# First sums staged in block tiles, and a weight add moved from VectorE to an accumulating DMA, in a Strassen-type feed-forward layer

## Chip, cores and metric

One core of a Trainium2 chip. The metric is the device time of one execution in microseconds; the time before is the median of 3 runs.

## What is computed (the reference, shortened)

One decoder layer on x of 512 tokens by 2048 features, in float32: a token mixer (gated linear attention beside differential attention), then a gated feed-forward with a causal convolution of width 3. The change touches only the feed-forward, and of it the passage from the up to the down projection and the down projection itself:

```python
def conv_ffn(h, w_ffn_in, conv_w, conv_b, w_ffn_out):    # h: (1, 512, 2048)
    up = h @ w_ffn_in                                    # 2048 x 11264
    a, b = up[..., :5632], up[..., 5632:]
    a = causal_conv3(a, conv_w) + conv_b
    return (gelu(a) * b) @ w_ffn_out                     # 5632 x 2048
x = x + rmsnorm(conv_ffn(rmsnorm(x, g2), ...), g3)
```

## The kernel before

**Products in two halves.** Every float32 operand is split in two: ScalarE copies it into a float32r tile (the high half, `whi`), VectorE subtracts that from the operand (the low half, `wlo`). A product is three matmuls: high by high, high by low, low by high. Weights are loaded, split and used in granules of 128 x 1024 words (512 KB); `granule` (line 116) does the split, on lines 125 and 126. The split tiles are a ring of six, three granules.

**Seven products for eight.** Both projections are cut into units that use a Strassen-type scheme: a unit has seven products instead of eight, named x0, z0, y0, z1, x1, y1, y2, each of two granules. Its weights are sums of blocks of the weight matrix, its other operands sums of blocks of activations. `class Unit` (line 209) runs them. `self.t` (two tiles tagged `rt`, a ring of four) holds block (0,0) for x0; then `more` (line 226) adds block (0,1) with an accumulating DMA from POOL, for z0; then VectorE adds block (1,1), which lies in `self.b22`, on line 267, for y0; then VectorE adds block (1,0), which lies in `self.b21`, on line 291, for y2. `self.b22` (two tiles tagged `raw`, also a ring of four) is read by z1, gets block (0,1) by another pair of accumulating DMAs, and is then `self.e`, for y1. `self.b21` is read by x1 and by the add on line 291.

**Units.** The up projection has 20 Strassen units (line 1376), the down projection 10 (`down_unit`, line 1356; two halves of the columns for each of five pairs of groups). The order of TensorE's work interleaves neighbours: y0, z1, x1, y1 of a unit, x0 of the next, y2 of the unit, z0 of the next. An up granule is 24 matmuls of 256 columns, a down granule 12 of 512 columns.

**Activation sums.** The down units read sums of activation blocks (a11, s5, s2, s3, a12, s7, a22), which the up stage has written to DRAM. `stage` (line 1331) loads one of them into a tile `st` of the pool `ff`; `prepare` (line 1335) splits it into a place in `ah` and `al` (lines 138 and 139), where the up stage's activations lay. For the first pair of groups this happens in the last up unit (lines 1384 to 1411). The pool `ff` takes the space of `sums`, whose last reader is z1 of that unit, so a tile `st` is free only then.

**Outputs.** A unit's product lies in PSUM banks; `into` (line 1350) takes it into the accumulators: ScalarE copies on line 1352 for the first pair of groups, VectorE adds on line 1354 for the others. x0's product is collected apart, in `accp`, and added to three quarters of the accumulators at the start of `last_group` (lines 1482 to 1487), twelve adds of 128 x 512. After it come the last group's plain products (lines 1470 to 1472), the norm and the output.

**Order.** Outside the stretches under `manual_schedule`, a list scheduler orders each engine's instructions when the kernel is built: it takes what is ready by its own estimate of time, the earlier line of the program first. Adds and loads can therefore run well ahead of the place in which they are written. All plain loads are issued on SP's queue, accumulating DMAs on POOL's; both queues are in order. `step` (line 95) takes work from the list `fill` after a granule, at a rate that `pace` sets.

Of the kernel before, what the change touches and what calls it, by code (L numbers as in the profile page):

```python
# [9 lines left out]
F32 = mybir.dt.float32  # L10
# [3 lines left out]
ALU = mybir.AluOpType  # L14
# [3 lines left out]
P = 128  # L18
# [12 lines left out]
GR = 1024  # L31
# [6 lines left out]
def hybrid_layer(ctx: ExitStack, tc: tile.TileContext, x, attn_pre_norm, w_in, w_alpha_up, b_alpha,  # L38
# [52 lines left out]
    fill = []  # L91
# [14 lines left out]
    def drain():  # L106
        while fill:
            for _ in fill.pop(0):
                pass
# [99 lines left out]
    class Unit:  # L209
        def __init__(self, a, block, prods, chain, out, narrow=True):  # L210
            self.narrow = narrow
            self.a, self.block, self.prods, self.chain, self.out = a, block, prods, chain, out
            self.banks, self.b22, self.b21, self.t, self.x_done = {}, None, None, None, False

# [8 lines left out]
                self.prods(self.banks[c], op, g, hl, seg[1] == "0")  # L223
                step()

        def more(self, raws, j):
            for g in range(2):
                nc.gpsimd.dma_start(out=raws[g].rearrange("p (a b) -> p a b", a=self.a),  # L228
                                    in_=self.block(0, j, g), accum_op=ALU.add)

        def ahead(self):
            self.e = [room["rt"].tile([P, GR], F32, name="rt", tag="rt", bufs=4) for _ in range(2)]
# [30 lines left out]
        def y0(self):  # L263
            if self.b22 is None:
                self.fetch()
            for g in range(2):
                tt(self.t[g], self.t[g], self.b22[g], ALU.add)
            self.run("y0", "s2", self.t)
            self.out("y0", self.banks["y"])

        def z1(self):
# [15 lines left out]
        def y1(self):  # L287
            self.run("y1", "s7", self.e)
            self.out("y1", self.banks["y"])
            for g in range(2):  # L290
                tt(self.t[g], self.t[g], self.b21[g], ALU.add)

        def y2(self):
# [1034 lines left out]

    staged = {}

    def stage(c, n):
        raw = staged[c, n] = ff.tile([P, GR], F32, name="st", tag="st", bufs=4)
        dma(raw, sd[c][n].rearrange("p g x -> p (g x)"))

    def prepare(c, n):
        if (c, n) not in staged:
            stage(c, n)
        split(piece(ah, *place[n]), piece(al, *place[n]), staged.pop((c, n)))
# [11 lines left out]
    def into(dst, b, sign, first):  # L1350
        if first:
            act(dst, b, AF.Copy, scale=float(sign))
        else:
            tt(dst, dst, b, ALU.add if sign > 0 else ALU.subtract)

    def down_unit(c, cb):
        def block(i, j, g):
            gi = 2 * c + 1 + g
            col = 1024 * cb + 512 * j
            return w_y3[:, 4 * gi + 2 * i:4 * gi + 2 * i + 2, col:col + 512]  # L1360

        def chain(ch):
            return [bank(psm if ch == "x" else psa) for _ in range(2)]

        def out(seg, b):
            for j in range(2):
                if seg == "x0":
                    into(accp[j][:, 512 * cb:512 * (cb + 1)], b[j], 1, c == 0)
                    continue
                half, col, sign = {"z0": (1, 1, 1), "y0": (0, 1, -1), "z1": (0, 1, 1), "x1": (0, 0, 1),  # L1370
                                   "y1": (1, 1, -1), "y2": (1, 0, 1)}[seg]
                into(quarter(acc[2 * half + j], 2 * cb + col), b[j], sign, c == 0 and seg in ("z0", "y0", "x1", "y2"))

        return Unit(2, block, down_prods, chain, out, narrow=False)

    ups = [up_unit(gi, br) for gi in range(1, NG) for br in range(2)]
    for i, u in enumerate(ups):
        nxt = ups[i + 1] if i + 1 < len(ups) else None
        if i == 0:
            u.x0()  # L1380
            u.z0()
        u.y0()
        u.z1()
        if nxt is None:
            sums.close()
            ff = ctx.enter_context(tc.tile_pool(name="ff", bufs=2, reuse_waits="tile"))
            for n in ("a11", "s5", "s2", "s3"):
                stage(0, n)
        if i == 0:
            for h, r in enumerate(s7raw):  # L1390
                split(up["s7"][0][:, h], up["s7"][1][:, h], r)
        if nxt is None:
            prepare(0, "a11")
            stage(0, "a12")
        u.x1()
        if nxt is None:
            prepare(0, "s5")
            stage(0, "s7")
        u.y1()
        if nxt is not None:  # L1400
            nxt.x0()
            u.y2()
            nxt.z0()
        else:
            downs = [down_unit(c, cb) for c in range(NG // 2) for cb in range(2)]
            prepare(0, "s2")
            stage(0, "a22")
            downs[0].x0()
            prepare(0, "s3")
            downs[0].fetch()  # L1410
            u.y2()
    accp = [ff.tile([P, D // 2], F32, name=f"accp{j}", bufs=1) for j in range(2)]
# [7 lines left out]
    def quarter(v, c):  # L1420
        return v[c // 2][:, 512 * (c % 2):512 * (c % 2 + 1)]
# [58 lines left out]
        eng.tensor_tensor(a, a, quarter(g3, c), ALU.mult)  # L1480

    def last_group(gi, us):
        for j in range(2):
            for half, c, op in ((1, 0, ALU.add), (1, 1, ALU.subtract), (0, 1, ALU.subtract)):
                for b in range(2):
                    dst = quarter(acc[2 * half + j], 2 * b + c)
                    tt(dst, dst, accp[j][:, 512 * b:512 * (b + 1)], op)
        for c in range(2):
            gr = ffn_out_weights(gi, c)
            for t in range(NT):  # L1490
                ffn_out_part(us, gr, t, c)
                gain(t, c, nc.vector)

        rs = {}
        x1 = {t: v[:, h].rearrange("p k c -> p (k c)").bitcast(F32)
              for t, (v, h) in enumerate(((ah, 1), (al, 1), (ah, 2), (al, 2)))}
        for t in range(NT):
            dma(x1[t], x1d[t])

        def finish(t, *ps):  # L1500
            for i in ps:
                sl = slice(512 * i, 512 * (i + 1))
                a = quarter(acc[t], i)
                stt(a, a, rs[t], x1[t][:, sl], ALU.mult, ALU.add)
                if t == 3:
                    dma(out2[t * P:(t + 1) * P, sl], a)
                elif i % 2:
                    sl = slice(512 * i - 512, 512 * (i + 1))
                    dma(out2[t * P:(t + 1) * P, sl], acc[t][i // 2])

        with tc.manual_schedule(engines=IN_ORDER):
            gr = [ffn_out_weights(gi, c) for c in (2, 3)]
            for t in range(NT):
                ffn_out_part(us, gr[0], t, 2)
                gain(t, 2, nc.gpsimd if t < 3 else nc.vector)
                if t:
                    finish(t - 1, 0, 1, 2)
                ffn_out_part(us, gr[1], t, 3)
                if t:
                    finish(t - 1, 3)  # L1520
                gain(t, 3, nc.vector)
                ss = small.tile([P, 1], F32, name="ss", tag="ss")
                nc.vector.reduce_sum(ss, ssf[t], axis=AX.X)
                rs[t] = rsqrt_mean(ss, D)
            finish(3, 0, 1, 2, 3)
# [40 lines left out]
```

## Time and profile before

| | |
|---|---|
| median of 3 runs | 2111.48 us (2108.53 to 2116.08) |
| the profiled execution | 2112.14 us, its span 2110.4 us |
| TensorE matmul busy | 2069.4 us (98%) |
| TensorE weight loads busy | 1892.6 us (90%) |
| VectorE busy | 1555.2 us (74%) |
| ScalarE busy | 967.9 us (46%) |
| DMA moved | 353.31 MB, mean 167 GB/s |

The last up unit's y2 and the first down unit's x0 lie at 1652 to 1665 us; the down units end near 2056, the output at 2110. In the rows below PE is TensorE, DVE VectorE, ACT ScalarE, POOL GpSimd and SP SyncE; a q behind an engine's name is its queue of DMA issues. L126 is line 126.

### The profile page before, as it was taken

The page shows a single profiled execution, that of the slowest core. Times are in us where ns is not written, and L with a number is a line of the kernel's source. Part 1 is how long each engine was busy: PE and PEld are TensorE (multiplying, and loading weights), DVE is VectorE, ACT ScalarE, POOL GpSimd, SP SyncE. Part 2 cuts the span into 40 slices and gives each one's busy share as a digit, 9 for nine tenths or more (in the row PEclk, how much of TensorE's full clock was granted, in tenths as well). Part 3 has the DMA queues.
Part 4 walks back from the last instruction along what each step waited for, and adds up shares of the span by engine and source line. Part 5 has one row for each costly group of instructions (what it writes and reads, how often), then busy time and mean ns, then how long its engine had stood idle before and what let it go on. Part 6 is the DMA issues. An engine that isn't in the chain of part 4 may idle for free.

```text
span 2110.4 us, 34792 instructions
## 1 busy us (share of the span) xinstructions
PE 2069.4 (98%) x14161; PEld 1892.6 (90%) x14161; DVE 1555.2 (74%) x1873; ACT 967.9 (46%) x1247; POOL 248.1 (12%) x281
## 2 busy tenths in 40 slices
PE   7999999999999999999999999999999999999997
PEld 5899999888888889899999999999999788887886
DVE  7957667577873255887787877878778777988887
ACT  4445444444553234454544444454455564444433
POOL 2010111111110000011111011111111110111101
PEclk9999999999999999999999999999999999999999
DMA  9376675844455245447667677577675876775753
GB/s 309 104 172 165 159 170 137 274 126 144 148 160 202 95 150 170 116 114 185 161 140 189 147 170 185 128 172 171 151 175 145 261 209 173 193 195 151 190 151 138
DMA packets 255269, 353.31 MB, mean 167 GB/s; under 512 B 14128, under 2 KB 185572, under 8 KB 253316
## 3 DMA queue, kind: packets, MB, share of 16 engines
q1 hardware_dynamic: 184260, 268.24, 37.4%
q0 software_dynamic: 70848, 82.85, 25.0%
q8 instruction: 111, 1.82, 0.3%
q14 instruction: 50, 0.41, 0.1%
HBM read 303.33 MB, written 47.71 MB: 166 GB/s over the span
## 4 chain that ended last, share of the span: by engine, by line
PE 32%; issue 22%; DVE 3%; DMA 2%; POOL 2%; ACT 0%; POOLq 0%; DVEq 0%; SPq 0%; ACTq 0%
PE bank L320 6%; PE bank L319 6%; PE bank L318 6%; PE bank L1346 3%; PE bank L1347 3%; PE bank L1348 3%; PE bank L164 1%; PE bank L163 1%; PE bank L162 1%; DMA rt<-in_w_ffn_out_dram 1%; DVE wlo L126 1%; POOL rt L228 1%; POOL raw L228 1%; PE bank L1471 0%; PE bank L1472 0%
## 5 line engine op out<-in xcount | busy, mean ns | idle before, releaser
L125 ACT ACTIVATE whi<-raw 128x1024 fp32r<-128x1024 f32 x283 | 298.9, 1061 | 494.6 <-PE bank L319 164.8
L126 DVE TENSOR_TENSOR wlo<-raw,whi 128x1024 fp32r<-128x1024 f32 x283 | 343.6, 1220 | 231.5 <-ACT whi L125 228.1
L125 ACT ACTIVATE whi<-rt 128x1024 fp32r<-128x1024 f32 x306 | 322.8, 1060 | 357.9 <-PE bank L319 198.6
L126 DVE TENSOR_TENSOR wlo<-rt,whi 128x1024 fp32r<-128x1024 f32 x306 | 373.1, 1221 | 141.9 <-ACT whi L125 132.8
L318 PE MATMUL bank<-ah,whi 128*128 128x256 f32 x1600 | 442.0, 276 | 0.9 <-DVE u L352 0.9
L320 PE MATMUL bank<-ah,wlo 128*128 128x256 f32 x1600 | 442.1, 276 | 0.3 <-DVE wlo L126 0.3
L319 PE MATMUL bank<-al,whi 128*128 128x256 f32 x1600 | 441.9, 276 | 0.0
L318 PEld LDWEIGHTS bank<-ah,whi 128*128 128x128 f32 x1600 | 300.4, 188 | 1.4 <-issue 1.0
L320 PEld LDWEIGHTS bank<-ah,wlo 128*128 128x128 f32 x1600 | 300.3, 188 | 0.8 <-DVE wlo L126 0.8
L319 PEld LDWEIGHTS bank<-al,whi 128*128 128x128 f32 x1600 | 300.3, 188 | 0.1
L1347 PE MATMUL bank<-wlo,ah 128*128 128x512 f32 x560 | 219.2, 391 | 1.4 <-DVE wlo L126 1.4
L1346 PE MATMUL bank<-whi,ah 128*128 128x512 f32 x560 | 213.7, 392 | 6.2 <-ACT whi L125 3.0
L1348 PE MATMUL bank<-whi,al 128*128 128x512 f32 x560 | 218.2, 390 | 0.0
L181 PE MATMUL bank<-whi,ah 128*128 128x512 f32 x448 | 184.5, 414 | 0.0
L182 PE MATMUL bank<-wlo,ah 128*128 128x512 f32 x448 | 175.2, 391 | 1.0 <-DVE wlo L126 0.8
L183 PE MATMUL bank<-whi,al 128*128 128x512 f32 x448 | 175.1, 392 | 0.0
L1346 PEld LDWEIGHTS bank<-whi,ah 128*128 128x128 f32 x560 | 105.2, 188 | 30.4 <-ACT whi L125 6.1
L1347 PEld LDWEIGHTS bank<-wlo,ah 128*128 128x128 f32 x560 | 105.5, 188 | 25.7 <-DVE wlo L126 4.0
L1348 PEld LDWEIGHTS bank<-whi,al 128*128 128x128 f32 x560 | 105.4, 188 | 21.7
L318 PE MATMUL bank<-s5h,whi 128*128 128x256 f32 x400 | 110.7, 277 | 1.1 <-ACT whi L125 1.0
L320 PE MATMUL bank<-s5h,wlo 128*128 128x256 f32 x400 | 110.6, 277 | 0.8 <-DVE wlo L126 0.8
L320 PE MATMUL bank<-s2h,wlo 128*128 128x256 f32 x400 | 110.8, 277 | 0.0
(283 smaller groups left out, 4406.9 us busy)
## 6 DMA issues: line engine op xcount, KB each, us to landing
raw<-in_w_ffn_in_dram SPq DMA_DIRECT2D x96, 512.0 KB, 5.2
raw<-in_w_in_dram SPq DMA_DIRECT2D x64, 512.0 KB, 4.6
raw<-in_w_ffn_out_dram SPq DMA_DIRECT2D x48, 512.0 KB, 5.6
rt<-in_w_ffn_in_dram SPq DMA_DIRECT2D x40, 512.0 KB, 5.8
rt<-in_w_ffn_in_dram POOLq DMA_DIRECT2D x40, 512.0 KB, 5.9
raw<-in_w_ffn_in_dram POOLq DMA_DIRECT2D x40, 512.0 KB, 7.0
raw<-in_w_o_dram SPq DMA_DIRECT2D x32, 512.0 KB, 3.8
rt<-in_w_ffn_out_dram SPq DMA_DIRECT2D x20, 512.0 KB, 8.3
```

What stands on the lines that cost most here:

```text
L125: act(hi, raw, AF.Copy)
L126: tt(lo, raw, hi.bitcast(F32), ALU.subtract)
L181: mm(banks[t], ah[:, t, s, :], w[0][:, k, :], start=st, stop=False)
L182: mm(banks[t], ah[:, t, s, :], w[1][:, k, :], start=False, stop=False)
L183: mm(banks[t], al[:, t, s, :], w[0][:, k, :], start=False, stop=sp)
L228: nc.gpsimd.dma_start(out=raws[g].rearrange("p (a b) -> p a b", a=self.a), in_=self.block(0, j, g), accum_op=ALU.add)
L318: mm(o, wh, sh[:, :, kk, :], start=start and kk == 0 and n == 0, stop=False, **NOW)
L319: mm(o, wh, sl[:, :, kk, :], start=False, stop=False, **NOW)
L320: mm(o, wl, sh[:, :, kk, :], start=False, stop=kk == HK - 1, **NOW)
L1346: mm(b[j], sh[:, o:o + P], w[0][:, q, :], start=start and st == 0, stop=False, **NOW)
L1347: mm(b[j], sh[:, o:o + P], w[1][:, q, :], start=False, stop=False, **NOW)
L1348: mm(b[j], sl[:, o:o + P], w[0][:, q, :], start=False, stop=st == 3, **NOW)
```

## The change

Three things. (1) In the last up unit, a11 and s5 are loaded into two tiles `rt` of the ring that holds unit blocks, right behind y0, and are split before x1; the first blocks of down unit 0 are loaded (`begin`) behind x1, and the remaining sums follow in another order. (2) In down units the add of block (1,0) on line 291 is left out; in its place `more` is called behind y0's granules, for an accumulating DMA. Up units and mixer units keep the add. (3) The twelve adds of `accp` are taken from `last_group` and put on the list `fill` in the last two down units.

```diff
         def __init__(self, a, block, prods, chain, out, narrow=True):
             self.narrow = narrow
+            self.aside = not narrow
...
-        def more(self, raws, j):
+        def more(self, raws, j, i=0):
             for g in range(2):
                 nc.gpsimd.dma_start(out=raws[g].rearrange("p (a b) -> p a b", a=self.a),
-                                    in_=self.block(0, j, g), accum_op=ALU.add)
+                                    in_=self.block(i, j, g), accum_op=ALU.add)
...
             self.run("y0", "s2", self.t)
+            if self.aside:
+                self.more(self.t, 0, 1)
             self.out("y0", self.banks["y"])
...
             self.out("y1", self.banks["y"])
-            for g in range(2):
+            for g in range(0 if self.aside else 2):
                 tt(self.t[g], self.t[g], self.b21[g], ALU.add)
...
-    def stage(c, n):
-        raw = staged[c, n] = ff.tile([P, GR], F32, name="st", tag="st", bufs=4)
+    def stage(c, n, raw=None):
+        if raw is None:
+            raw = ff.tile([P, GR], F32, name="st", tag="st", bufs=4)
+        staged[c, n] = raw
         dma(raw, sd[c][n].rearrange("p g x -> p (g x)"))
...
+    def shares(b):
+        for half, c, op in ((1, 0, ALU.add), (1, 1, ALU.subtract), (0, 1, ALU.subtract)):
+            for j in range(2):
+                dst = quarter(acc[2 * half + j], 2 * b + c)
+                tt(dst, dst, accp[j][:, 512 * b:512 * (b + 1)], op)
+                yield
...
                     into(accp[j][:, 512 * cb:512 * (cb + 1)], b[j], 1, c == 0)
+                    if c == NG // 2 - 1 and j:
+                        fill.append(shares(cb))
+                        pace[0], pace[1] = 0.65, 0.0
...
         u.y0()
+        if nxt is None:
+            for n in ("a11", "s5"):
+                stage(0, n, rp.tile([P, GR], F32, name="rt", tag="rt", bufs=4))
         u.z1()
         if nxt is None:
             sums.close()
             ff = ctx.enter_context(tc.tile_pool(name="ff", bufs=2, reuse_waits="tile"))
-            for n in ("a11", "s5", "s2", "s3"):
+            for n in ("a11", "s5"):
+                prepare(0, n)
+            for n in ("s2", "s3"):
                 stage(0, n)
...
-        if nxt is None:
-            prepare(0, "a11")
-            stage(0, "a12")
         u.x1()
         if nxt is None:
-            prepare(0, "s5")
-            stage(0, "s7")
+            downs = [down_unit(c, cb) for c in range(NG // 2) for cb in range(2)]
+            downs[0].begin()
+            for n in ("a12", "s7"):
+                stage(0, n)
+            for n in ("s2", "s3"):
+                prepare(0, n)
         u.y1()
...
         else:
-            downs = [down_unit(c, cb) for c in range(NG // 2) for cb in range(2)]
-            prepare(0, "s2")
             stage(0, "a22")
             downs[0].x0()
-            prepare(0, "s3")
             downs[0].fetch()
             u.y2()
...
     def last_group(gi, us):
-        for j in range(2):
-            for half, c, op in ((1, 0, ALU.add), (1, 1, ALU.subtract), (0, 1, ALU.subtract)):
-                for b in range(2):
-                    dst = quarter(acc[2 * half + j], 2 * b + c)
-                    tt(dst, dst, accp[j][:, 512 * b:512 * (b + 1)], op)
+        drain()
```

## Rows read from the trace of the kernel before

**Rows 1.** The page, part 1: busy us (share of the span) xinstructions.

```profile
PE 2069.4 (98%) x14161; PEld 1892.6 (90%) x14161; DVE 1555.2 (74%) x1873; ACT 967.9 (46%) x1247; POOL 248.1 (12%) x281
```

**Rows 2.** Windows: us; PE, PEld, DVE, ACT, POOL busy; PEclk, DMA share, GB/s.

```profile
1600.00:1650.00 50.00, 50.00 (x444) 50.00 (x443) 35.14 (x37) 24.27 (x28) 5.16 (x4) 1.00 0.75 187
1700.00:1750.00 50.00, 50.00 (x222) 41.42 (x221) 36.51 (x36) 28.10 (x34) 4.83 (x4) 1.00 0.78 204
1652.20:1692.30 40.10, 34.44 (x159) 26.60 (x158) 32.89 (x33) 21.16 (x25) 4.78 (x4) 0.96 0.87 260
```

**Rows 3.** PE's waits, 1652 to 1692.3: us in total, times, longest us.

```profile
PE bank L1346 <- ACT whi L125: 3.0, 2, 2.1
PE bank L1347 <- DVE wlo L126: 1.4, 3, 0.7
```

**Rows 4.** PE's waits, 1692.3 to 2060.

```profile
PE bank L1346 <- DVE acc L1354: 2.3, 3, 1.2
PE bank L1471 <- DVE wlo L126: 1.1, 1, 1.1
```

**Rows 5.** Timeline, 1612 to 1674, of SP, ACT, DVE, POOL: start us, us, instruction.

```profile
1616.57 3.49 SPq L50 DMA_DIRECT2D rt<-in_w_ffn_out_dram  x2
...
1641.51 0.50 SPq L50 DMA_DIRECT2D st<-sd0a  x1
...
1649.80 1.06 ACT L138 ACTIVATE ah<-st 128x1024 fp32r<-128x1024 f32 x1 [2.94 <-DMA st<-sd0a]
...
1670.48 1.06 ACT L125 ACTIVATE whi<-rt 128x1024 fp32r<-128x1024 f32 x1 [4.39 <-DMA rt<-in_w_ffn_out_dram]
...
1629.04 1.21 DVE L291 TENSOR_TENSOR rt<-rt,raw 128x1024 f32<-128x1024 f32 x1
...
1652.04 1.22 DVE L126 TENSOR_TENSOR wlo<-rt,whi 128x1024 fp32r<-128x1024 f32 x1
...
1653.55 1.19 POOL L228 DMA_DIRECT2D rt<-in_w_ffn_out_dram  x1 [14.45 <-DVE wlo L126]
1656.95 1.20 POOL L228 DMA_DIRECT2D rt<-in_w_ffn_out_dram  x1 [2.21 <-DVE wlo L126]
```

**Rows 6.** DMA issues at 1653.55, 1656.95 and 2028.02: KB, us to landing.

```profile
rt<-in_w_ffn_out_dram POOLq DMA_DIRECT2D x1, 512.0 KB, 10.9
...
rt<-in_w_ffn_out_dram POOLq DMA_DIRECT2D x1, 512.0 KB, 13.5
...
raw<-in_w_ffn_out_dram POOLq DMA_DIRECT2D x1, 512.0 KB, 5.8
```

**Rows 7.** Groups by line, DVE, 1692 to 2060: count, busy us, mean ns, idle before.

```profile
L291 DVE TENSOR_TENSOR rt<-rt,raw 128x1024 f32<-128x1024 f32 x18 | 21.9, 1219 | 0.1
...
L1487 DVE TENSOR_TENSOR acc<-acc,accp 128x512 f32<-128x512 f32 x8 | 5.2, 680 | 0.0
```

**Rows 8.** Windows: a full and a resting stretch of the DMA engines.

```profile
1640.00:1672.00 32.00, 28.14 (x195) 24.81 (x194) 19.08 (x18) 15.96 (x18) 2.39 (x2) 0.99 1.02 321
...
2014.00:2030.00 16.00, 16.00 (x72) 13.23 (x72) 16.00 (x19) 7.21 (x7) 1.19 (x1) 1.00 0.05 9
```

**Rows 9.** DMA queues, and one of POOL's two issue groups, 1692 to 2050.

```profile
q1 hardware_dynamic: 19422, 45.35, 36.0%
q0 software_dynamic: 9797, 18.88, 33.0%
...
raw<-in_w_ffn_out_dram POOLq DMA_DIRECT2D x18, 512.0 KB, 6.9
```

**Rows 10.** Timeline of the last down unit: DVE, POOL, ACT, PE.

```profile
2023.04 1.21 DVE L126 TENSOR_TENSOR wlo<-rt,whi 128x1024 fp32r<-128x1024 f32 x1
...
2031.82 1.20 POOL L228 DMA_DIRECT2D raw<-in_w_ffn_out_dram  x1 [2.60 <-DVE wlo L126]
...
2040.84 1.06 ACT L125 ACTIVATE whi<-raw 128x1024 fp32r<-128x1024 f32 x1 [5.87 <-DMA raw<-in_w_ffn_out_dram]
...
2043.96 0.39 PE L1346 MATMUL bank<-whi,ah 128*128 128x512 f32 x1
```

## The prediction

> **What bounds the kernel now.** I read the page's busy table first: TensorE is busy 98% of the span [rows 1]. So only idle and slowed matmuls can be won, and the next view is windows of 50 us. In the up stage and in a quiet part of the down stage TensorE is busy 50.00 of 50 [rows 2]; these give the pitch at which it works when nothing is late: 50/444 = 0.1126 us for a 256-column matmul, 50/222 = 0.2252 us for a 512-column one. The exception is the passage from the last up unit to the first down unit. In 40.1 us it ran 159 matmuls [rows 2], of which 48 are the last up unit's y2 (two granules of 24) and 111 are long: 48 x 0.1126 + 111 x 0.2252 = 30.4 us of work, so **9.7 us are lost there**. Of these 5.66 are idle (40.10 - 34.44); the rest are matmuls that restart or run slowly: the granted clock averages 0.96 in the stretch, so part of it ran at 1.2 GHz instead of 2.4, after TensorE had stood still for up to 2.1 us [rows 2, 3].
>
> The waits view names what ended that idle time: halves that ScalarE or VectorE had not yet split [rows 3]. From 1692 to 2060 the same view has only 2.3 us for sums that VectorE had not yet taken out of a bank (three times, the longest 1.2) and 1.1 us for a low half at the start of the tail [rows 4]. So all that the change can touch is 9.7 + 2.3 + 1.1 = 13.1 us, 0.6% of the time. What a measurement of this kernel can tell from no change is about 0.3%, 6.3 us; the change has to remove about half of all stalls to be seen.
>
> **The chain in the passage.** The timeline shows it [rows 5]. The first sums (a11, s5 and two more) can be loaded only at 1641.51, when z1 has read the last tile whose space they take. Their load lands at 1649.8: ScalarE waits 2.94 us for it, splits a11, and only then splits the first granule of x0. VectorE ends that granule's low half at 1653.26. Behind it POOL issues the accumulating DMA that makes z0's weights, at 1653.55 and 1656.95. They need 10.9 and 13.5 us to land, while one that runs alone needs 5.8 [rows 6]: from 1640 to 1672 the DMA engines are full, share 1.02 [rows 8]. ScalarE gets z0's second granule at 1670.48 after 4.39 us of waiting, and TensorE stands still before it.
>
> **Change, part 1: staging in the block tiles.** The tiles are free early: the first loads of down unit 0 enter them at 1616.57 and about 3 us later [rows 5]. The change swaps the two pairs of loads: a11 and s5 go there, and unit 0's block loads come when their splits have read the tiles. Moved are 4 DMAs on SP's queue, 2 splits on ScalarE and 2 on VectorE (1.22 us each, as the low half at 1652.04). Landing by about 1625, the sums can be split while z1 runs. VectorE is dense there, but two adds of line 291, wanted only by y2, stand in that stretch (one is shown at 1629.04 [rows 5]); the two low halves now come earlier in the program and can take their places, so I cost the splits at nothing; without that cover they delay z1 by up to 2.4 us. Unit 0's blocks then load from about 1630 and 1636; on SP the first sums' loads of before stood at 1641.51, and what stands behind the blocks now is not wanted sooner, so I cost SP's order at nothing.
>
> What x0 gains: ScalarE was free at 1649.80 - 2.94 = 1646.86, so x0's first split, which stands straight behind a11's (1649.80 + 1.06), can start about 4 us earlier, the second about 5, since more sums' splits stood ahead of it. POOL then issues at about 1649.6 and 1652. With the old latencies the weights land at 1660.5 and 1665.5, and are split 2.3 us later (1.06 + 1.22): 1662.8 and 1667.8. Undisturbed, TensorE wants them at 1652.2 + 24 x 0.2252 + 48 x 0.1126 = 1663.0 and 2.7 later, 1665.7. So the first is in time and the second 2.1 us late, or not late at all if its latency falls toward 5.8. The DMA engines stay full (the transfers change places, they don't vanish), so I take 1.5 us, and 1.2 for what comes after it (y0's weights wait on VectorE for the same granule). Of 9.7 us 2.7 stay: **7.0 us won**, between 2.0 (blocks late, see below) and 9.7.
>
> **Part 2: the last weight add as a DMA.** Gone are 20 adds of line 291, 18 of them in the rows (21.9 us, 1.22 each [rows 7]). VectorE is filled without a gap where they stand: 16.00 of 16 us from 2014 to 2030 [rows 8], with two of them inside. Each of the three waits for a bank is at most 1.2 us [rows 4], the two adds of a unit are 2.4, so these waits should go: 2.3 us. Of the 1.1 at the tail's start I take 0.2, since that low half stands behind the late end of the last e granule [rows 10], which the change doesn't touch. **2.5 us won**, between 0 and 3.4.
>
> Added are 20 accumulating DMAs on POOL's queue, issued when y0's splits have read the tile and wanted by y2, eight granules (8 x 12 x 0.2252 = 21.6 us) later; their own landing, even 13.5 us, is hidden. What they cost is the engines. In the down stage 36 such DMAs (18 on each ring of tiles) hold 33.0% of 358 us [rows 9]: 3.3 us each, so a unit's two are 6.6 us, and the stage's share goes from 69% to 87%. They stand right ahead of z1's pair (the e blocks) in POOL's queue, and y1 waits for that pair. Against this: they fall into the one stretch of a unit in which the DMA engines rest (share 0.05 from 2014 to 2030 [rows 8]). In the last unit, y0's second low half ends at 2024.25 [rows 10], the first some 2.3 earlier, so the new pair is through by about 2022 + 5.8 + 3.3 = 2031.1. The e pair, issued up to 2.4 us earlier than now (no adds ahead of z1's low halves), would follow by 2037.7 if alone, and with plain loads beside it (now 3 us) by about the time at which ScalarE gets it now, 2040.84 [rows 10]. So I cost it at 1.0 us in all, between 0 and 18.
>
> By the Trainium skill, "DMA: Bandwidth & Descriptors", section on the anatomy of one DMA, such a transfer would take 2.0 us plus its bytes over 436 GB/s, 3.2 us, and hold the engines for 1.2 only. The measured 5.8 alone is nearly twice that and decides here; by the page's figure the new pair would cost nothing and the sum would be 1.0 lower.
>
> **Part 3: the shares.** Twelve adds of 0.68 us (eight of them in [rows 7], four on other tiles) change their place in the program, not their number. They already run in VectorE's gaps: they are counted before 2060, ahead of the tail that they are written in. I cost the move at nothing; a badly placed one delays a low half by 0.68.
>
> **Sum.** -7.0 - 2.5 + 1.0 = -8.5 us. The profiled execution took 2112.14 (its span of 2110.4 and 1.7 around it), which gives 2103.6; it lies 0.66 above the median of the runs shown, so 2103.0.
>
> **Rivals.** *The extra DMAs become the wait (slower).* Place: y1's second granule in each down unit. Today POOL issues its DMA at 2031.82, ScalarE takes it at 2040.84 and TensorE begins the granule at 2043.96, when its low half has just ended: under 1 us to spare [rows 10]. If the plain loads move into the same stretch (a tile that line 291 used to hold is free sooner), the new 6.6 us are not absorbed: less 2.4 and less 0.8, up to 3.4 us per unit. At 2 us in nine units it is 18 us: 2112.1 - 9.5 + 18 = 2120.6. It decides as soon as the e pair lands 1 us later behind its split than now. For it: latencies of 13.5 against 5.8 under load [rows 6]. Against: the resting stretch [rows 8]. The Trainium skill's rule in the same page, under "Issuing engines are not separate DMA queues", that DMAs from any queue share the same 16 engines, speaks for this rival; rows 6 agree with it.
>
> *The stall only moves (same).* The tiles are no spare ones: unit 0's blocks lose the early place. If a11 and s5 are split only around 1640, the blocks load into the full stretch, land near 1650, and x0 is as late as now; z0's DMAs too. Then only 2.0 of the 9.7 is won, the two splits of 1.0 (s5 and the sum after it) that no longer stand ahead of x0's second granule: 2112.1 - 2.0 - 2.5 + 1.0 = 2108.6, against the median 2108. For it: the DMA share of 1.02; against: VectorE has the places of line 291.
>
> *All stalls go (faster than forecast).* 2112.1 - 9.7 - 3.4 = 2099.0, if the second accumulating DMA needs less than 11.4 us and the new ones hide.
>
> **How the numbers follow.** Forecast 0.45 (2101 to 2106 with its own bounds), all gone 0.13, only moved 0.27, slower 0.15. Below 2111.5 - 6.3 = 2105.2 lie the sweep and all but the edge of the forecast: 0.56. Within 0.3%: 0.29. Slower: 0.15. The range runs from 2097 (the sweep, with the runs' own scatter) to 2113, which leaves out most of the slower case and little else.
>
> **What would show it.** Right: a11's split before 1640; z0's accumulating DMAs issued by 1652; the passage's loss below 4 us and no clock dip; no bank wait on line 1354; in each unit four accumulating DMAs in the stretch that was empty. Wrong: unit 0's block loads landing after 1648; TensorE waiting in y1 or z0 on ScalarE, and that on a DMA, in most units; waits inside z1 of the last up unit.

## The result, and the profile after

The changed kernel takes 2122.79 us (median of 7 runs, 2119.27 to 2126.37) against 2111.48 of the kernel before beside it: ratio 1.0056, 95% interval 1.0043 to 1.0068. It is **slower by 11.3 us**; the forecast was 8.5 us faster, and the range ended at 2113. The profiled execution took 2120.76 us.

The page of the changed kernel, busy times and DMA queues:

```profile
PE 2074.1 (98%) x14161; PEld 1893.4 (89%) x14161; DVE 1532.9 (72%) x1853; ACT 966.0 (46%) x1247; POOL 271.9 (13%) x301
...
q1 hardware_dynamic: 184260, 268.24, 37.1%
q0 software_dynamic: 76288, 93.33, 27.6%
```

VectorE has lost its 20 adds (22 us less than in [rows 1]), POOL has 20 issues more. TensorE is as busy as before, over a longer span. Windows of the changed kernel (columns as in [rows 2]) say where:

```profile
1700.00:1750.00 50.00, 48.67 (x211) 38.88 (x209) 31.86 (x30) 26.42 (x33) 7.19 (x6) 1.00 0.85 221
1652.20:1692.30 40.10, 36.46 (x178) 29.59 (x177) 27.64 (x29) 18.53 (x23) 6.01 (x5) 1.00 1.02 290
...
1754.00:1773.00 19.00, 18.31 (x81) 14.76 (x80) 11.60 (x13) 6.15 (x7) 4.77 (x4) 1.00 0.91 196
```

The passage has improved: 178 matmuls instead of 159 in the same 40.1 us, at full clock. The quiet part of the down stage, 50.00 of 50 in [rows 2], now has 11 matmuls fewer. The third line is a stretch of the third down unit in which the DMA engines are nearly full (share 0.91). The kernel before, in the same unit, up to the issue of z1's pair and in the same 19 us:

```profile
1750.00:1760.00 10.00, 10.00 (x46) 8.29 (x45) 9.87 (x10) 6.91 (x9) 0.22 (x1) 1.00 0.22 82
1754.00:1773.00 19.00, 19.00 (x85) 15.63 (x84) 15.58 (x17) 9.19 (x10) 2.39 (x2) 1.00 0.64 166
```

TensorE's waits in the two stretches of [rows 3, 4]:

```profile
PE bank L1351 <- ACT whi L125: 2.8, 3, 1.6
PE bank L1352 <- DVE wlo L126: 0.8, 1, 0.8
...
PE bank L1352 <- DVE wlo L126: 6.7, 10, 0.8
PE bank L1351 <- DVE acc L1359: 3.9, 5, 2.3
PE bank L1351 <- ACT whi L125: 0.7, 2, 0.4
```

(L1351 to L1353 are the down matmuls, L1359 is the accumulators' add.) The first two lines are the passage, the last three the units behind it. Ten waits of at most 0.8 us for a low half are the mark of a granule that arrives at the last moment: its first matmul runs on the fresh high half, and the second waits for the low half, which VectorE ends 1.2 us later. In the one shown below (1775.50) the wait is 0.76 us; start to start, the second matmul is 1.03 us later than one pitch.

**One unit, followed.** The third down unit, POOL, ScalarE and TensorE of the changed kernel:

```profile
1754.02 1.19 POOL L229 DMA_DIRECT2D rt<-in_w_ffn_out_dram  x1 [15.66 <-DVE wlo L126]
1755.55 1.20 POOL L229 DMA_DIRECT2D rt<-in_w_ffn_out_dram  x1 [0.34 <-issue]
1757.69 1.19 POOL L229 DMA_DIRECT2D raw<-in_w_ffn_out_dram  x1 [0.95 <-DVE wlo L126]
1760.02 1.20 POOL L229 DMA_DIRECT2D raw<-in_w_ffn_out_dram  x1 [1.14 <-DVE wlo L126]
...
1769.06 1.06 ACT L125 ACTIVATE whi<-raw 128x1024 fp32r<-128x1024 f32 x1 [8.56 <-DMA raw<-in_w_ffn_out_dram]
1773.13 1.06 ACT L125 ACTIVATE whi<-raw 128x1024 fp32r<-128x1024 f32 x1 [3.01 <-DMA raw<-in_w_ffn_out_dram]
...
1771.43 0.50 PE L1352 MATMUL bank<-wlo,ah 128*128 128x512 f32 x1 [0.69 <-DVE wlo L126]
1775.50 0.50 PE L1352 MATMUL bank<-wlo,ah 128*128 128x512 f32 x1 [0.76 <-DVE wlo L126]
```

The DMA view gives issue to landing of these four, one by one, and of the whole stage (1692 to 2050) the software queue and z1's pairs:

```profile
rt<-in_w_ffn_out_dram POOLq DMA_DIRECT2D x1, 512.0 KB, 6.3
...
rt<-in_w_ffn_out_dram POOLq DMA_DIRECT2D x1, 512.0 KB, 9.8
...
raw<-in_w_ffn_out_dram POOLq DMA_DIRECT2D x1, 512.0 KB, 11.3
...
raw<-in_w_ffn_out_dram POOLq DMA_DIRECT2D x1, 512.0 KB, 13.0
...
q0 software_dynamic: 14688, 28.32, 47.6%
...
raw<-in_w_ffn_out_dram POOLq DMA_DIRECT2D x18, 512.0 KB, 10.8
```

The new pair (`rt`) is issued first and z1's pair (`raw`) right behind it. They land at 1760.3, 1765.4, 1769.0 and 1773.0, some 4 us apart: one after another. z1's pair, which y1 needs, took 6.9 us in [rows 9] and takes 10.8 now (medians; in this unit 5.9 and 7.8 before, 11.3 and 13.0 now). ScalarE waits for it, and TensorE for the split.

Adding up how much later than one pitch each down matmul begins gives 12.3 us for the kernel before and 23.2 for this one, 12.2 of them in y1, where the kernel before had none. These 12.2 lie in the first five units (4.7 in the first) and the seventh; the other four lose nothing in y1.

### The profile page after: what moved, and what is told of

Its sections match the earlier page's. It is cut to its first block, busy times and chain, and to the rows that moved or that the text cites. A ratio compares the mean times of both kernels' runs of the same rounds, so it can differ in the third digit from the quotient of the medians.

```text
span 2119.0 us, 34814 instructions
## 1 busy us (share of the span) xinstructions
PE 2074.1 (98%) x14161; PEld 1893.4 (89%) x14161; DVE 1532.9 (72%) x1853; ACT 966.0 (46%) x1247; POOL 271.9 (13%) x301
## 4 chain that ended last, share of the span: by engine, by line
issue 45%; PE 7%; DMA 4%; POOL 4%; DVE 1%; ACT 0%; POOLq 0%; DVEq 0%; ACTq 0%; SPq 0%
DMA rt<-in_w_ffn_out_dram 3%; POOL rt L229 2%; POOL raw L229 2%; PE bank L1351 2%; PE bank L1352 1%; PE bank L1353 1%; DMA raw<-in_w_ffn_out_dram 1%; PE bank L1489 0%; PE bank L1490 0%; PE bank L1488 0%; DVE u L1518 0%; PE bank L164 0%; PE bank L162 0%; PE bank L163 0%; DMA st<-ud 0%
## 5 line engine op out<-in xcount | busy, mean ns | idle before, releaser
L1351 PE MATMUL bank<-whi,ah 128*128 128x512 f32 x560 | 217.5, 393 | 7.2 <-DVE acc L1359 3.9
L1353 PE MATMUL bank<-whi,al 128*128 128x512 f32 x560 | 218.6, 391 | 0.0
L1351 PEld LDWEIGHTS bank<-whi,ah 128*128 128x128 f32 x560 | 105.3, 188 | 34.1 <-ACT whi L125 8.9
L1353 PEld LDWEIGHTS bank<-whi,al 128*128 128x128 f32 x560 | 105.6, 189 | 21.6
L323 PE MATMUL bank<-s3h,wlo 128*128 128x256 f32 x400 | 110.6, 277 | 0.0
```

The costliest lines, as they stand in the source:

```text
L323: mm(o, wl, sh[:, :, kk, :], start=False, stop=kk == HK - 1, **NOW)
L1351: mm(b[j], sh[:, o:o + P], w[0][:, q, :], start=start and st == 0, stop=False, **NOW)
L1353: mm(b[j], sl[:, o:o + P], w[0][:, q, :], start=False, stop=st == 3, **NOW)
```

## The experiments

"Lead" below is how much earlier than in the kernel before a matmul begins, both counted from the same up matmul near 1627 us; "at y0" means the first matmul of that product's second granule. Every kernel was timed beside the kernel before, whose median was 2111.6 to 2112.8. Leads and losses are read from one profiled execution of each kernel.

### The parts alone

**Part 1 alone** (the staging; the shares' adds stay in `last_group`). Against the changed kernel:

```diff
-            self.aside = not narrow
+            self.aside = False
```

> Part 1 alone on the kernel before: a11 and s5 staged in the block tiles, the adds of line 291 and the shares as they were. Theory (the staging wins what its passage shows, the accumulating DMAs give it back): TensorE's loss between the up and the down stage falls from about 10 us to under 3, the down units keep the loss of before (some 4.5 us), time 2111.5 - 8 = 2103 to 2105. Rival (the staging itself upsets the order of what follows): the down units lose 10 us or more, time 2112 to 2122.

2114.3 us, ratio 1.0008 (0.9998 to 1.0018): no gain. Its loss in the passage did fall, and its lead was 6.2 us at y0 of the first unit; it was 2.1 at z0 of the third unit, 0.1 at z0 of the fourth, and at the end the kernel was 2.8 behind. Waits from 1692.3 to 2060:

```profile
PE bank L1352 <- DVE wlo L126: 3.4, 6, 0.8
PE bank L1351 <- DVE acc L1359: 3.2, 4, 1.2
```

The bank waits of [rows 4] are still there, and the six waits of at most 0.8 us for a low half are new. Neither theory as put holds: the staging wins in the passage about what was expected, and gives it back in the next units.

**Part 2 alone** (the accumulating pair).

```diff
             self.run("y0", "s2", self.t)
+            if self.aside:
+                self.more(self.t, 0, 1)
...
-            for g in range(2):
+            for g in range(0 if self.aside else 2):
                 tt(self.t[g], self.t[g], self.b21[g], ALU.add)
```

> Part 2 alone on the kernel before: each down unit's last weight add as two accumulating DMAs issued behind y0's splits, nothing staged otherwise. Theory (the new pair stands ahead of z1's pair in the DMA queue, and y1 waits for that): y1's granules are split behind a landing in most units, TensorE loses about 18 us more in the down units, time 2111.5 + 18 = 2129 (2122 to 2133). Rival (staging or moved shares make the loss): 2109 to 2113.

2126.87, ratio 1.0071 (1.0055 to 1.0087), 14.8 us slower: the theory's case. Its waits from 1692.3 to 2060 are of the changed kernel's kinds, and longer in sum:

```profile
PE bank L1350 <- DVE wlo L126: 9.1, 13, 0.8
PE bank L1349 <- DVE acc L1357: 3.8, 5, 2.1
PE bank L1349 <- ACT whi L125: 2.1, 4, 1.0
```

**Part 3 alone** (the shares, on the kernel before).

```diff
+                    if c == NG // 2 - 1 and j:
+                        fill.append(shares(cb))
+                        pace[0], pace[1] = 0.65, 0.0
...
     def last_group(gi, us):
-        for j in range(2):
...
+        drain()
```

> Part 3 alone on the kernel before: the twelve adds of the shares handed out during the last two down units. Both theories: no change, 2110 to 2113. If the bank waits in the changed kernel on VectorE's adds, the longest of them 2.3 us, come from these adds, 2114 or more.

2112.49, ratio 1.0003 (0.9994 to 1.0013): nothing, as expected.

### What the adds on VectorE were worth

```diff
-            for g in range(2):
+            for g in range(2 if self.narrow else 0):
                 tt(self.t[g], self.t[g], self.b21[g], ALU.add)
```

> The kernel before without the twenty adds of line 291 and with nothing in their place: y2 uses a weight tile that lacks its last term. It prices the adds alone. Theory (they cause the three bank waits of the down stage, 2.3 us): 2108 to 2110.5. Rival (VectorE's adds are covered wholly): 2111.5 to 2112.5. Rival (a tile that comes free sooner pulls loads forward into the full stretch): 2113 or more.

2105.8, ratio 0.9972 (0.9962 to 0.9981): **6.4 us** faster (4.0 to 8.0 by the interval), more than the theory asked. From 1692.3 to 2060 TensorE waits for nothing at all in this trace. The stage, columns as in [rows 2]:

```profile
1692.00:2050.00 358.00, 358.00 (x1581) 296.45 (x1580) 289.57 (x306) 173.40 (x176) 43.02 (x36) 1.00 0.70 185
```

So the relief was worth some two and a half times the 2.5 us in the sum, and the accumulating pair in its place costs 14.8 + 6.4, about 21 us.

### Place in the queue

**Written behind z1's pair**, in the changed kernel:

```diff
             self.run("y0", "s2", self.t)
-            if self.aside:
-                self.more(self.t, 0, 1)
...
                 self.more(self.e, 1)
+            if self.aside:
+                self.more(self.t, 0, 1)
```

> The changed kernel with one step moved: the new accumulating pair is issued behind z1's pair instead of ahead of it. Same DMAs, same bytes. Theory (place in the queue): y1 gets its granules as in the kernel before, y2 has time for its own; TensorE's added loss in the down units falls from 18 us to under 4, time 2101 to 2107. Rival (the share of the engines, 87% instead of 69%, whatever the order): the pair only hits another granule, y2 or the next z0, time 2117 to 2123.

2124.91, ratio 1.0072 (1.0059 to 1.0085), a little above the rival's range. It tells nothing of the place: the scheduler issues what is ready, and the new pair still came first (in one unit at 1715.59, z1's at 1718.32 and 1719.74). So an edge was added that holds it behind:

```diff
-                self.more(self.e, 1)
+                last = self.more(self.e, 1)
+                if self.aside:
+                    with tc.issue_after(last.ins):
+                        self.more(self.t, 0, 1)
...
```

(`more` now returns its last transfer, and the call in `y0` is gone.)

**Part 2 alone with the edge.**

> Part 2 alone, with an edge that makes the new pair issue behind z1's pair (in the run before that asked for this, the scheduler still issued it first, because its tile was ready first). Same transfers as in part 2 alone, which took 2126.9. Theory (place in POOL's queue): z1's pair lands 6 to 8.5 us after issue as in the kernel before, instead of 10 to 13; TensorE's loss in y1 falls from 14 us to under 4; time 2109 to 2115. Rival (the DMA engines' time, whatever the order): z1's pair stays late or y2 and z0 take over the loss; 2121 to 2128.

2122.46, ratio 1.005 (1.0034 to 1.0065). By the adding up of above, y1 loses 0.0 us instead of 14.2, yet the time is the rival's. The DMA view from 1692 to 2050, one plain load, and the waits from 1692.3:

```profile
raw<-in_w_ffn_out_dram SPq DMA_DIRECT2D x37, 512.0 KB, 10.5
...
raw<-in_w_ffn_out_dram POOLq DMA_DIRECT2D x18, 512.0 KB, 7.1
...
st<-ud SPq DMA_DIRECT2D x1, 512.0 KB, 15.4
...
PE bank L1351 <- DVE acc L1359: 8.9, 5, 7.4
PE bank L1352 <- DVE wlo L126: 2.3, 4, 0.8
```

z1's pair is back at 7.1 (6.9 before). Now the plain loads are late: 10.5 us instead of 5.3. One of them, a first operand of the last group (`ud`), took 15.4 instead of 5.2; ScalarE waited 13.0 us for it, VectorE 10.2 for ScalarE, and an accumulator's add stood behind that split on VectorE: TensorE stopped once for 7.4 us in the eighth unit, and its granted clock from 1985 to 1995 is 0.66: y2 of that unit loses 9.8 us. Another part of the loss lies before the first unit's y0, where this kernel is 0.9 us behind the kernel before and part 2 alone was 2.5 ahead.

**The whole change with the edge.**

> The whole change with the same edge. Theory of the place in the queue, with the staging's gain given back in the first two down units as in the staging alone: 2109 to 2115. If the staging's gain of about 6 us is kept once VectorE has no adds: 2103 to 2107. Rival (the engines' time): 2117 to 2126.

2127.21, ratio 1.0067 (1.0052 to 1.0083), slower than all three cases allow, the rival's by the least. It is the same stop in the eighth unit (longest wait 7.3 us, behind another wait of 13.0 us for `ud`), and 5.7 us of lead go at the start of the tail, where TensorE waits 3.6 us for ScalarE.

**The edge, and the pair, in the second to seventh units only**, adds on VectorE in the other four:

```diff
         nxt = downs[i + 1] if i + 1 < len(downs) else None
+        u.aside = 1 <= i <= 6
```

> The whole change, the pair issued behind z1's pair, but only in the second to seventh units; the other four add on VectorE as before. Theory (place in POOL's queue makes the loss in y1; the rest of that run's loss stood in the first and the eighth unit): those units lose under 6 us together, none of it in y1; time 2104 to 2111. Rival (two accumulating transfers a unit are too much for the engines wherever they stand): 2114 to 2122.

2110.65, ratio 0.9993 (0.9984 to 1.0002). The six units lose 2.7 us together (3.2 in the kernel before), none of it in y1: the theory's case. Place in the queue does make the loss in y1. The long stop in the eighth unit is gone with the pair (its y2 loses 2.4 us instead of 9.0 in the whole change with the edge). But even in the right place the gain is small: the time is that of the kernel before, and against part 1 alone (ratio 1.0008) the intervals still overlap.

### The price of an accumulating transfer

**The pair as plain loads**, at the same place, of the same size:

```diff
-                self.more(self.t, 0, 1)
+                for g in range(2):
+                    dma_aside(self.t[g].rearrange("p (a b) -> p a b", a=self.a), self.block(1, 0, g))
```

> The changed kernel with the new pair as ordinary loads on POOL's queue, at the same place and of the same size, that overwrite the tile instead of adding to it (y2 multiplies that block alone). Theory (the price is the accumulating transfer's hold on the engines, 3.3 us of all sixteen for 512 KB against about 1.5 for a plain load): the pair delays z1's by 3 us instead of 7, y1 loses under 4 us, time 2108 to 2114. Rival (two more transfers ahead in that queue cost the same whatever they do): 2119 to 2125.

2106.01, ratio 0.9976 (0.9964 to 0.9988): faster than before, more than the theory asked; y1 loses 2.2 us instead of 12.2. One such load alone (issued at 1983.16), and the stage:

```profile
rt<-in_w_ffn_out_dram POOLq DMA_DIRECT2D x1, 512.0 KB, 4.1
...
q0 software_dynamic: 12388, 28.32, 40.8%
...
raw<-in_w_ffn_out_dram POOLq DMA_DIRECT2D x18, 512.0 KB, 8.8
```

The software queue moves the same 28.32 MB in this stretch as the changed kernel and holds the engines 40.8% instead of 47.6%. Against the 33.0% of [rows 9], 18 plain loads hold all sixteen for (0.408 - 0.330) x 358 / 18 = 1.6 us each. An accumulating one holds them for 3.3 by [rows 9], and by the same difference, in the changed kernel, for (0.476 - 0.330) x 358 / 18 = 2.9. The factor is 1.9 to 2.1, about two. The Trainium skill, "Collectives: The Full Stack", in the section on the bandwidth ceiling, has a reason for such a factor in a collective: the add of a reducing transfer needs two source reads, so it puts two read descriptors where a copy puts one; it measured 1.93. The factor here, of a load added onto a tile, agrees with that; the descriptors themselves no run here shows.

**One accumulating transfer per unit**, the other granule added on VectorE:

```diff
             if self.aside:
-                self.more(self.t, 0, 1)
+                self.more(self.t, 0, 1, 1)
...
-            for g in range(0 if self.aside else 2):
+            for g in range(1 if self.aside else 0, 2):
                 tt(self.t[g], self.t[g], self.b21[g], ALU.add)
```

(`more` gets a fourth argument, the number of granules.)

> The changed kernel with one accumulating transfer per down unit instead of two: the first granule of the tile by DMA, the second by an add on VectorE as before (10 transfers, 10 adds). One accumulating transfer holds the engines 3.4 us, as long as the two plain loads of the run before (3.6). Theory (the engines' time decides): z1's pair as late as with the plain loads, y1 loses under 4 us, half of VectorE's relief is kept, time 2107 to 2112. Rival (an accumulating transfer ahead in the queue costs by itself): y1 loses 6 us or more, time 2114 to 2119, half way between part 1 alone and the changed kernel.

**2104.16, ratio 0.9963 (0.995 to 0.9975)**, with nothing left out of the computation, 8.0 us under the kernel before and 18.6 under the changed one. Waits from 1692.3 to 2060, POOL in the third unit, the landings of its last two, and the stage:

```profile
PE bank L1352 <- DVE wlo L126: 0.8, 1, 0.8
...
1750.23 1.19 POOL L229 DMA_DIRECT2D rt<-in_w_ffn_out_dram  x1 [14.84 <-DVE wlo L126]
1754.93 1.20 POOL L229 DMA_DIRECT2D raw<-in_w_ffn_out_dram  x1 [3.51 <-DVE wlo L126]
1757.27 1.19 POOL L229 DMA_DIRECT2D raw<-in_w_ffn_out_dram  x1 [1.14 <-DVE wlo L126]
...
raw<-in_w_ffn_out_dram POOLq DMA_DIRECT2D x1, 512.0 KB, 7.0
...
raw<-in_w_ffn_out_dram POOLq DMA_DIRECT2D x1, 512.0 KB, 8.1
...
q0 software_dynamic: 12240, 23.60, 41.5%
...
raw<-in_w_ffn_out_dram POOLq DMA_DIRECT2D x18, 512.0 KB, 6.3
```

One transfer holds the engines about as long as two plain loads (41.5% and 40.8% of the stage; by the working above 3.4 us for the one and 3.1, not 3.6, for the two), and it is nearly through when z1's pair is issued 4.7 and 7.0 us behind it. z1's pair lands in 6.3, and TensorE waits once; y1 loses 2.8 us, all in the first unit. That is faster than the theory's case: half the adds gone give the whole relief as far as this can be told (below).

**The same with the edge from the second unit on** (the transfer is issued in z1 as above, where `u.behind` is set):

```diff
         nxt = downs[i + 1] if i + 1 < len(downs) else None
+        u.behind = i > 0
```

> The same with the one transfer issued behind z1's pair in the second to tenth units (the first as in the run beside it). Theory (engines' time): no loss in y1 at all, but the same time to within 2 us of the run beside it. Rival (place in the queue matters at any amount): 3 us or more below the run beside it.

2106.29 (0.9965 to 0.9984 of before), 2.1 us above the run beside it with overlapping intervals: not the rival's gain of 3. At this amount no effect of the place can be told.

**The same on the kernel before**, without staging and shares.

> One accumulating transfer per unit on the kernel before, without staging and moved shares. If the staging is worth 2 us once VectorE has fewer adds (2105.8 against 2103.4 without any): 2 us above the first run of this call. If the staging is worth nothing here: the same time.

2105.67 (0.9954 to 0.9979): 1.5 above the first, less than this measurement can tell. It is also the time of the kernel without any of the adds, 2105.8: within the intervals, ten adds fewer are as good as twenty.

**The same, but with both adds on VectorE in the first unit.**

```diff
     downs[0].z0()
+    downs[0].aside = False
```

> The half version (2104.2) with both adds on VectorE in the first unit. Theory (its 2.8 us in the first unit's y1 are the transfer in the stretch where the engines are full): 2101 to 2103. Rival (that loss is the lead of the staging being taken back by the landings, whatever is added): 2104 to 2106.

2104.04 (0.9948 to 0.9972): the rival's case. The first unit's y1 still loses 1.6 us; the new transfer was not its cause alone.

### What takes the staging's lead back

**Part 1 without the adds** (part 1 alone, and the edit that took the adds out).

> Part 1 alone and without the adds of line 291 (y2 uses a weight tile that lacks its last term). Part 1 alone was 6.2 us ahead at y0 of the first unit and lost that by the third. Theory (VectorE's chain in the first units takes the lead back; without the adds it keeps it): 2099 to 2102, that is 6 under the kernel without the adds alone (2105.8). Rival (the landings of the block loads take it back, whatever VectorE does): 2104 to 2108.

2103.38 (0.9947 to 0.9975), 2.4 under the kernel without the adds alone: between the two cases, and the two intervals overlap, so the times alone don't show that the staging still wins something. Leads over the kernel before, in us, from the traces:

```
                          y0 of     z0 of the units       last
                          unit 1    3rd   4th   7th    granule
changed kernel              6.7     0.2  -3.3  -7.2     -10.2
part 1 alone                6.2     2.1   0.1  -1.0      -2.8
no adds                     0.8     1.7   1.8   2.9       6.7
part 1, no adds             5.9     4.0   4.1   5.1       9.0
half, before                1.3     2.5   1.5   2.5       6.4
half, changed               5.8     3.4   3.1   4.1       8.0
```

In every row that starts near 6, some 2 us or more are gone by the third unit; the rest is kept only where VectorE has fewer adds and no full pair takes their place. The two differences in the last column between rows with and without the staging are 2.3 and 1.6.

**Five staged sums loaded short**, on part 1 alone:

```diff
-        dma(raw, sd[c][n].rearrange("p g x -> p (g x)"))
+        src = sd[c][n].rearrange("p g x -> p (g x)")
+        if c == 0 and n in ("s2", "s3", "a12", "s7", "a22"):
+            dma(raw[:, :128], src[:, :128])
+            staged[c, n] = raw[:, None, :128].to_broadcast([P, 8, 128])
+        else:
+            dma(raw, src)
...
```

> Part 1 alone, with the five later first sums of the first group (s2, s3, a12, s7, a22) loaded as 128 columns instead of 1024 and split from those columns repeated: the same splits, 2.2 MB fewer to load between 1640 and 1700 us; the products with these sums are others. Part 1 alone was 6.2 us ahead of the kernel before at y0 of the first unit and 0.1 ahead at the end of the third. Theory (the bytes of the passage bind, so the gain is given back): the lead stays at 5 us or more, time 2105 to 2109. Rival (the order of the later units gives it back, not the bytes): the lead is gone by the third unit as before, 2111 to 2115.

2114.33 (0.9998 to 1.0021), and no answer: the instructions came in another order, ScalarE waited 7.07 us for z0's weights and TensorE 4.9 for ScalarE, and there was no lead whose fate could be followed. That the bytes of the passage take the first 2 us back is therefore only argued.

### The adds on GpSimd

```diff
-                tt(self.t[g], self.t[g], self.b21[g], ALU.add)
+                (tt if self.narrow else nc.gpsimd.tensor_tensor)(self.t[g], self.t[g], self.b21[g], ALU.add)
```

> The kernel before with the twenty adds of line 291 on GpSimd instead of VectorE: the same data, no new DMA. Theory (the adds on VectorE cost 6 us, as their removal without replacement showed, and GpSimd is busy 12%): 2105 to 2108. Rival (a GpSimd add holds up the accumulating DMAs that are issued behind it, or slows VectorE while it runs): 2110 to 2118.

2142.02, ratio 1.0142 (1.0123 to 1.016): 30 us slower, far beyond the rival's range. Both of the rival's ways show in the trace; what each of them costs was not separated. Groups by line, 1692 to 2060, and POOL in one unit:

```profile
L291 POOL TENSOR_TENSOR rt<-rt,raw 128x1024 f32<-128x1024 f32 x18 | 53.1, 2953 | 135.0 <-DVE wlo L126 135.0
...
L126 DVE TENSOR_TENSOR wlo<-rt,whi 128x1024 fp32r<-128x1024 f32 x72 | 96.1, 1340 | 26.2 <-ACT whi L125 26.0
L126 DVE TENSOR_TENSOR wlo<-raw,whi 128x1024 fp32r<-128x1024 f32 x53 | 79.9, 1517 | 41.5 <-ACT whi L125 40.2 <-PE bank L1348 1.3
...
1760.92 6.79 POOL L291 TENSOR_TENSOR rt<-rt,raw 128x1024 f32<-128x1024 f32 x2 [15.22 <-DVE wlo L126]
1769.34 1.20 POOL L228 DMA_DIRECT2D raw<-in_w_ffn_out_dram  x1 [1.62 <-issue]
```

An add takes 2.95 us there; a VectorE low half rises from 1.22 to 1.34 and 1.52 on average, and z1's pair is issued behind both adds.

**The changed kernel with GpSimd adds instead of the pair.**

> The changed kernel with the new accumulating pair replaced by GpSimd adds (staging and moved shares stay). If both gains hold and add up: 2099 to 2103. If only the relief of VectorE holds: 2104 to 2108. If GpSimd's add is in the way: 2110 or more.

2134.98, ratio 1.0115 (1.0098 to 1.0133): the third case, GpSimd's add in the way.

## Why the prediction was wrong

**The step that failed** is in part 2: "So I cost it at 1.0 us in all, between 0 and 18." The pair costs about 21 us (part 2 alone against the kernel without the adds). The stretch of rest and the times that were set against the cost came from the last down unit, where no next unit's loads run beside it and where the changed kernel, too, loses nothing. For it the text let the pair be through 3.3 us after its first transfer landed, and z1's pair follow "if alone". In a middle unit the kernel before rests for some 10 us at a share of 0.22 (1750 to 1760), not for 16 at 0.05. In the third unit the four transfers land one after another, 3.6 to 5.1 us apart, and over the stage z1's pair lands 4 us later behind its issue.

That was the slower rival, with its place (y1's granules, behind the new pair) and its mechanism, transfers that are not absorbed. The run with the edge adds something that the rival did not have: with the place put right y1 loses nothing, and the time stays. The engines' time for two transfers a unit then comes out elsewhere, at the plain loads.

The rival's time, 2120.6, is that of the profiled execution, 2120.76, by luck and out of other parts: it had 18 us of cost and 9.5 of gain, where the runs give about 21, and 6.4 + 3.5 (what staging and shares take off part 2 alone, 14.8 - 11.3; the intervals of these two overlap). It had the chance 0.15. The condition on which it was to decide, "as soon as the e pair lands 1 us later behind its split than now", could have been worked out from [rows 9]: one more accumulating transfer ahead holds the engines for 3.3 us, two for 6.6. The resting stretch was weighed by its length, and not by whether the pair that y1 waits for is in the same queue behind it.

**Part 2's gain** was mis-sized the other way: 2.5 us between 0 and 3.4, measured 6.4. The waits of [rows 4] were counted as the profile's idle time, 2.3; counted start to start, the units behind the first lose 3.3 in the kernel before. The first unit gained too (1.7 us of lead at z0 of the third unit), and so did the tail's start, 1.4 us of lead where the sum took 0.2.

**Part 1** was right in the passage and wrong in what follows. a11 is split at 1620.30 (wanted before 1640), the pair for z0's weights is issued at 1650.01 and 1654.14 (forecast 1649.6 and 1652) and lands at 1659.5 and 1663.9 (1660.5 and 1665.5), there is no clock dip, and the lead at y0 is 6.7 us where 7.0 was forecast. But it was costed as if the next units could keep it, and in the changed kernel all but 0.2 of it was gone by the third unit; part 1 alone had 2.1 left there and none at the end. "The stall only moves" came out here in its result and not in its mechanism: unit 0's blocks were issued from 1622.65, not into the full stretch, and the stall came back in the units behind. The two low halves costed at nothing do hold up z1 of the last up unit: counted from the up matmul near 1627, x0 begins 0.9 us later than before in the changed kernel and 1.7 in part 1 alone (with one wait of 0.6 us), inside the 2.4 that the text allowed.

**Part 3** was right: nothing.

**What would show it.** Of the signs named as right, a11's early split and the full clock came. The second of z0's DMAs was issued 2 us late, without harm. The passage's loss, counted as in the prediction, is 40.1 - 48 x 0.1126 - 130 x 0.2252 = 5.4 us and not below 4; 3.6 of it is already y1 of the first down unit. The bank waits did not go: five, with 3.9 us. The longest, 2.3 us at 1984.02, is VectorE again, held by a split whose sum landed late: ScalarE waited 4.08 us for `ud` there, hardly more than before, but the unit had no time to spare. After that stop TensorE ran at 1.2 GHz for some 3.4 us, an estimate from the granted clock of 0.86 from 1978 to 1990: 12 x 0.14 / 0.5. Of the signs named as wrong, "TensorE waiting in y1 or z0 on ScalarE, and that on a DMA, in most units" is the trace after: six units of ten lose time in y1.

## What to carry to other kernels

An add handed to an accumulating DMA is not free on the DMA side: here it held all engines about twice as long as a plain load of its size, and what was issued next on the same queue landed later by 4 us in the median, so ask who waits for that before asking whether the engines rest. Read the slack in a middle unit, not in the last one. If a full move costs more than it frees, try half of it: here the relief of VectorE needed only half, and half fitted into the queue. And time won in a passage can be lost again in the next units: of some 6 us won here at most 4 were left by the third unit, and what took the first 2 was not shown.

## What was not expected of the hardware

An accumulating transfer of 512 KB held the sixteen engines for 2.9 to 3.4 us where a plain one on the same queue held them for 1.6, and landed in 5.8 us alone against 4.1. Beside queued accumulating transfers the plain loads of SP's queue can suffer as well: the median of the larger group (`raw`) rose from 5.3 to 10.5 us in part 2 alone with the edge, although the stage's share was not full (0.80); in the changed kernel, at the same share, it was 6.0. A GpSimd add of two 128 x 1024 tiles took 2.95 us, 2.4 times VectorE's, and VectorE's low halves in that stage were 10 and 24% longer on average.
